# Convolution in eight tiles, a later place for it, and a searched order of all queues, in a hybrid encoder block

## The chip, the cores and the metric

The kernel runs on the 8 cores of one Trainium2 chip. Each core takes one of 8 sequences, and no core talks to another. The time is device microseconds (us) of the slowest core. Some executions fall into a slower state, in which the cores of a die (cores 0 to 3 or 4 to 7) show a lower granted clock. The granted clock is the share of its full clock that TensorE was given. Medians are over all executions.

## The reference, cut to what matters

Per core: 2048 tokens of width 1024. One block does:

```python
x   = layer_norm(x)
u   = x @ W_in            # [q | k | v | conv-GLU halves | gates], 3840 columns
y_a = windowed_gqa(q, k, v) @ W_attn_out     # 8 heads, 128-token blocks, 3 key blocks each
glu = u_a * sigmoid(u_b)                     # 512 channels
dw  = depthwise_conv(glu, width 31) + b      # each channel alone, taps t-15 .. t+15
y_c = silu(layer_norm(dw)) @ W_conv_out
mix = (sigmoid(g_a) * y_a + sigmoid(g_c) * y_c) @ W_out
h   = layer_norm(alpha * x + mix)
out = layer_norm(alpha * h + (silu(h @ W_gate) * (h @ W_up)) @ W_down)   # D_FF = 2816
```

## The kernel before

The kernel is a list of operations. A helper records each with what it reads and writes, an estimated cost and a number called rank. A small list scheduler then simulates the engines: whenever an engine is free, it takes the ready operation of lowest rank. The resulting order of each queue is fixed in the program. Tokens are worked in four chunks of 512.

The convolution runs on TensorE. The GLU output goes to DRAM scratch and comes back as copies shifted by one token each, so that the 128 rows of the array hold 32 channels times 4 shifts, and a matmul of 128 rows by 32 columns applies 4 taps to 32 channels:

```python
def spread(c):                         # four loads of 540 KB for each chunk
    for s in range(4):
        load(shv[32*s:32*s+32, :, :], gs[:, :, c*512+s : c*512+s+GW], ..., rank=0.1*c)

def conv(c):
    for cc in range(4):                # four groups of 128 channels
        b = ring("conv", CONV)         # a fixed few PSUM banks for each purpose
        def f_conv(e, cc=cc, b=b):
            for m in range(8):         # 8 steps of 4 taps
                for q in range(4):     # 4 tiles of 32 columns
                    e.matmul(bank(b)[32*q:32*q+32, :], tapv[:, 4*cc+q, m, :],
                             shv[:, 4*cc+q, 4*m:4*m+512], start=(m == 0), stop=(m == 7))
        ...
for c in range(4):
    rank(100*c - 85); [ln_tile(t) for t in range(4*c, 4*c+4)]
    rank(100*c + 20); glu blocks of chunk c; glu_out(c)
    if c >= 1:
        rank(100*c + 10); spread(c - 1)
        rank(100*c + 35); conv(c - 1)
    rank(100*c + 60); kv(c)
    ...
rank(345); conv(3)
rank(370 + 5*c): q projections;   rank(400 + 20*c), but 330 for chunk 0: attention;   rank(500 + 100*c): gates
```

At the start, the eight weight loads of the GLU wait for x tile 0, and x tile 4 waits for the sixth of them:

```python
wop.append(castload(wA[4 + i], win_d[10 + i], ..., after=[xop[0]]))
xload(t, after=[wop[5]] if t == 4 else [])
```

The softmax here doesn't subtract the row's maximum and nothing guards it: scores larger than these inputs give would overflow.

## Time and profile before

| | before |
|---|---|
| median of 5 executions | 942.27 us (939.13 to 967.92) |
| profiled execution, slowest core (core 5) | 939.7 us; the cores lie between 925.3 and 939.7 |
| TensorE busy, core 5 | 885.1 us, so 54.6 us idle |
| convolution matmuls | 512, busy 34.8 us, with 14.0 us of waits just before them |

TensorE is the bound. The table of windows of core 5 shows where it falls short; its columns are the stretch, its length, then busy us of PE (TensorE), PEld (its weight loads), DVE (VectorE), ACT (ScalarE) and POOL (GpSimd) with their instructions, the granted TensorE clock, the DMA share and GB/s.

```profile
0.00:60.00 60.00, 45.04 (x297) 29.65 (x298) 45.87 (x82) 26.92 (x44) 15.16 (x30) 0.97 0.91 196
60.00:190.00 130.00, 111.84 (x962) 54.38 (x964) 64.33 (x98) 60.85 (x84) 31.06 (x31) 0.93 0.61 118
190.00:345.00 155.00, 147.12 (x1048) 68.94 (x1041) 110.50 (x151) 91.56 (x117) 47.85 (x50) 1.00 0.40 83
345.00:520.00 175.00, 170.81 (x822) 78.67 (x820) 76.20 (x108) 45.10 (x62) 46.63 (x67) 0.98 0.58 100
```

The four stretches leave 15, 18, 8 and 4 us of TensorE idle; from 520 to 900 us it is 1. In the second the clock is down to 0.93, so part of its busy time is slow work as well. That is the stretch of the convolutions.

### The profile page before, as it was taken

How to read it: one execution, taken by the hardware profiler on the slowest of the kernel's cores; microseconds unless marked ns; L12 is line 12 of the kernel's file. 1: busy time of each engine (PE TensorE's matmuls, PEld its weight loads, DVE VectorE, ACT ScalarE, POOL GpSimd, SP SyncE). 2: the span in 40 equal slices, each digit the busy share in tenths (PEclk: the TensorE clock that was granted, in tenths of full speed). 3: DMA queues.
4: the chain of work that ended last, by engine and by line, in shares of the span. 5: the costliest groups of instructions: out<-in, count | busy, mean ns of one | idle time of the engine just before them, and what ended most of it. 6: DMA issues, size and time to landing. Idle time of an engine off the chain costs nothing.

```text
span 939.7 us, 14653 instructions; the slowest of 8 cores (925.3 to 939.7 us)
## 1 busy us (share of the span) xinstructions
PE 885.1 (94%) x5067; PEld 419.2 (45%) x5067; DVE 495.3 (53%) x708; ACT 282.0 (30%) x397; POOL 221.4 (24%) x294
## 2 busy tenths in 40 slices
PE   5897987897999999998999999999999999999996
PEld 2653444443444444443444444444444444444442
DVE  7885324668777574424343386542685443622145
ACT  3562634588565223321222002231003220011100
POOL 3210330551231422334220013320133310233000
PEclk9998998999999999999899999999999999999998
DMA  8965539527034700469982139660258721199201
GB/s 174 213 170 106 116 75 200 98 49 132 1 69 143 148 3 1 90 111 192 171 142 36 35 112 174 107 112 12 91 126 144 126 42 34 46 162 164 44 24 67
DMA packets 46970, 95.43 MB, mean 102 GB/s; under 512 B 5425, under 2 KB 15793, under 8 KB 46641
## 3 DMA queue, kind: packets, MB, share of 16 engines
q0 software_dynamic: 27360, 54.57, 36.3%
q1 hardware_dynamic: 19538, 39.93, 15.9%
q8 instruction: 42, 0.69, 0.3%
q14 instruction: 30, 0.25, 0.1%
HBM read 138.52 MB, written 10.52 MB: 159 GB/s over the span
## 4 chain that ended last, share of the span: by engine, by line
PE 77%; DMA 12%; DVE 4%; issue 3%; SPq 2%; ACT 1%; POOL 0%; DVEq 0%; ACTq 0%; POOLq 0%
PE ps L967 30%; PE ps L985 16%; PE ps L596 13%; PE ps L913 6%; PE ps L862 5%; PE ps L683 3%; DMA sh<-glu_scratch 3%; DMA xE<-x 3%; DMA xt<-x 2%; SPq L479 2%; DMA bias<-biasT 2%; DMA glu_scratch<-glus 2%; DMA wA<-win 1%; PE ps L799 1%; DVE E L471 1%
## 5 line engine op out<-in xcount | busy, mean ns | idle before, releaser
L967 PE MATMUL ps<-mT,wE 128*128 128x512 bf16 x1408 | 310.4, 380 | 0.6 <-DMA wE<-wg 0.6
L967 PEld LDWEIGHTS ps<-mT,wE 128*128 128x128 bf16 x1408 | 137.6, 98 | 165.0 <-issue 2.7
L457 ACT ACTIVATE sgb<-ps 128x512 f32<-128x512 f32 x88 | 52.5, 598 | 384.6 <-PE ps L967 310.0
L985 PE MATMUL ps<-wdn,hid 128*128 128x512 bf16 x704 | 152.6, 379 | 1.0 <-DVE hid L475 1.0
L475 DVE TENSOR_TENSOR hid<-ps,sgb 128x512 bf16<-128x512 f32 x88 | 60.8, 691 | 172.0 <-PE ps L967 153.5
L596 PE MATMUL ps<-x0T,wG 128*128 128x512 bf16 x512 | 118.7, 379 | 0.2 <-ACT gt L457 0.2
L985 PEld LDWEIGHTS ps<-wdn,hid 128*128 128x128 bf16 x704 | 68.8, 98 | 84.3 <-issue 1.5
L471 DVE SCALAR_TENSOR_TENSOR xE<-xE,ps 128x512 f32<-128x512 f32 x64 | 43.9, 686 | 86.1 <-PE ps L985 62.2
L509 POOL TENSOR_TENSOR rs<-mv,neghalf 128x1 f32<-128x1 f32 x28 | 35.1, 1254 | 186.3 <-DVE mv L507 186.3
L596 PEld LDWEIGHTS ps<-x0T,wG 128*128 128x128 bf16 x512 | 48.7, 98 | 60.0 <-issue 4.0
L457 ACT ACTIVATE gt<-ps,hbg 128x512 f32<-128x512 f32 x64 | 43.9, 686 | 87.6 <-PE ps L596 61.0
L471 DVE SCALAR_TENSOR_TENSOR E<-ps,bias 128x1024 f32<-128x1024 f32 x46 | 56.1, 1220 | 20.1 <-PE ps L799 15.6
L471 DVE SCALAR_TENSOR_TENSOR t<-gt,ps 128x512 f32<-128x512 f32 x64 | 43.4, 682 | 43.5 <-ACT gt L457 34.2
L475 POOL TENSOR_TENSOR mT<-t,t 128x512 bf16<-128x512 f32 x32 | 43.4, 1358 | 96.0 <-DVE t L471 76.9
L483 POOL DMA_DIRECT2D wE<-wg x70 | 37.9, 542 | 115.6 <-PE ps L967 103.5
L596 PE MATMUL ps<-x0T,wA 128*128 128x512 bf16 (+1 forms) x320 | 60.1, 346 | 2.6 <-ACT x0T L462 2.5
L913 PE MATMUL ps<-wout,mT 128*128 128x512 bf16 x256 | 58.4, 381 | 0.0
L457 ACT ACTIVATE pT<-E 128x1024 bf16<-128x1024 f32 x46 | 48.3, 1057 | 33.7 <-DVE E L471 33.6
L483 POOL DMA_DIRECT2D wE<-wu x70 | 37.5, 536 | 63.8 <-PE ps L967 55.8
L683 PE MATMUL ps<-sh,tapw 128*32 128x512 bf16 x512 | 34.8, 434 | 14.0 <-DMA sh<-glu_scratch 12.9
L496 DVE BATCH_NORM_STATS2 st<-xE 128x6 f32<-128x512 f32 x64 | 44.4, 694 | 6.1
L596 PEld LDWEIGHTS ps<-x0T,wA 128*128 128x128 bf16 x320 | 31.6, 101 | 27.6 <-issue 4.8
(98 smaller groups left out, 808.7 us busy)
## 6 DMA issues: line engine op xcount, KB each, us to landing
wE<-wg POOLq DMA_DIRECT2D x70, 256.0 KB, 5.6
wE<-wu POOLq DMA_DIRECT2D x70, 256.0 KB, 5.8
sh<-glu_scratch SPq DMA_DIRECT2D x16, 540.0 KB, 10.9
xt<-x SPq DMA_DIRECT2D x16, 512.0 KB, 8.0
xE<-x SPq DMA_DIRECT2D x16, 512.0 KB, 4.5
out<-xE SPq DMA_DIRECT2D x15, 512.0 KB, 2.7
wdn<-wd POOLq DMA_DIRECT2D x11, 512.0 KB, 5.6
wG<-win POOLq DMA_DIRECT2D x16, 256.0 KB, 10.6
```

Source lines behind the costliest of these rows:

```text
L457: sc.add("act", lambda e: e.activation(out, in_, func, **kw), reads=reads, writes=writes, cost=c, table=table, **k)
L471: sc.add("dve", lambda e: e.scalar_tensor_tensor(out, in0, scalar, in1, op0, op1), reads=reads, writes=writes, cost=dcost(n), **k)
L475: sc.add(eng, lambda e: e.tensor_tensor(out, a, b, op), reads=reads, writes=writes, cost=dcost(n) if eng == "dve" else 0.1 + n * 0.0023, **k)
L483: return sc.add("pool", lambda e: e.dma_start(out=dst, in_=src), reads=reads, writes=writes, dma=True, cost=0.6, nbytes=nbytes, **k)
L496: sc.add("dve", lambda e, h=h: e.bn_stats(st[:, 6 * h:6 * h + 6], src[:, 512 * h:512 * h + 512]), reads=[regs[h]], writes=[(sk, h)], cost= ...
L509: sc.add("pool", lambda e: e.tensor_tensor(rs_out, var, neghalf[:, 0:1], ALU.pow), reads=[mreg, "neghalf"], writes=[rreg], cost=0.7)
L596: ins = e.matmul(bank(b)[:, 0:n], w8(w)[:, kc, :], x0v(c)[:, kc, s0:s0 + n], start=(kc == 0), stop=(kc == 7))
L683: ins = e.matmul(bank(b)[32 * q:32 * q + 32, :], tapv[:, 4 * cc + q, m, :], shv[:, 4 * cc + q, 4 * m:4 * m + 512], start=(m == 0), stop=(m ...
L862: ins = e.matmul(bank(b), wv[:, x, f * 128:(f + 1) * 128], src[:, x, :], start=(x == 0), stop=(x == 3))
L913: ins = e.matmul(bank(h), mv[:, kc, tl * 128:(tl + 1) * 128], woutv[:, kc, h * 512:(h + 1) * 512], start=(kc == 0), stop=(kc == 7))
L967: ins = e.matmul(bank(b), w8(wE[i])[:, kc, :], hT[:, kc, :], start=(kc == 0), stop=(kc == 7))
L985: ins = e.matmul(bank(b), hidv[:, k, tl * 128:(tl + 1) * 128], wdnv[k // 2][:, k % 2, h * 512:(h + 1) * 512], start=(k == 0), stop=(k == N ...
```

## The change

The intent is to close the gaps of TensorE in the first 345 us. Five things are done at once.

1. The convolution uses 64 by 32 tiles, eight at a time: two shifts of 32 channels to a half of the rows, sixteen steps. Shifted loads halve to 271 KB. Matmuls come in groups of 32 with two banks.
2. The convolution and the k/v projections (but those of chunk 0) get ranks of 322 to 329, so that the GLU projections go first; the first attention has 330.
3. At the start, weights and x tiles no longer wait for each other, nor the q/k/v weights wQ for those of the GLU; ScalarE takes the statistics of 12 instead of 7 tiles; the GLU of chunks 0 and 1 goes by single tiles of 128 tokens.
4. Banks of PSUM, the memory that the matmuls write to, are picked by the scheduler from all eight, for each tile, instead of from fixed rings; its cost model is finer.
5. A table of 471 numbers, by their look found by a search, replaces or shifts the ranks, and a few loads are moved by hand at the head of the queues.

Smaller parts: the zeros of the padding are set by a memset instead of two strided writes, the convolution's output has a second buffer, and the loads of gate weights wait for the last x tile.

```diff
+RANK = { ("att0", "pe"): 3.31, ("att1", "act"): 1.58, ...      # about 100 lines of searched ranks
+    "conv0": 238.3, "conv1": 315.05, "conv2": 323.77, "conv3": 324.65, ... }
-        op.rank = self.cur if rank is None else rank
+        op.rank = RANK.get(self.group, self.cur) + RANK.get((self.group, eng), 0) if rank is None else rank
@@ start
-        wop.append(castload(wA[4 + i][:, :], win_d[10 + i], ["wA%d" % (4 + i)], after=[xop[0]]))
+        wop.append(castload(wA[4 + i][:, :], win_d[10 + i], ["wA%d" % (4 + i)], wire=1.72))
-            xload(t, after=[wop[5]] if t == 4 else [])
-        if t % 2 and t > 1:
+        if t % 4:
             act_stats(...)
@@ spread: copies for two halves of the rows, two shifts each
+        for h in range(2):
+            for s in range(2):
+                load(shv[64*h+32*s : 64*h+32*s+32, :, lo:hi], gs[:, 8*h:8*h+8, c*512+s+lo : c*512+s+hi], ...)
@@ conv
-            b = ring("conv", CONV)
+        for p in range(2):
+            bs = [T("conv"), T("conv")]
+            for m0 in range(0, 16, 4):
+                def f_conv(e, p=p, bs=bs, m0=m0):
+                    for m in range(m0, m0 + 4):
+                        for q in range(4):
+                            for h in range(2):
+                                e.matmul(pb(bs[h])[32*q:32*q+32, :], tapv[64*h:64*h+64, 4*p+q, m, :],
+                                         shv[64*h:64*h+64, 4*p+q, 2*m:2*m+512], start=(m == 0), stop=(m == 15))
@@ ranks
-            rank(100 * c + 35)
+            stage("conv%d" % (c - 1), 321 + c)
             conv(c - 1)
-        rank(100 * c + 60)
+        stage("kv%d" % c, 326 + c if c else 60)
         kv(c)
-    rank(345)
+    stage("conv3", 325)
     conv(3)
@@ after the scheduler: hand-set heads of queues, and all but 4 of 26 warm-up groups dropped
+    for name, at in {"small": 1, "xt0": 2, "xt1": 3}.items(): move("sp", find("sp", name)[0], at)
+    names = ["wA4", "wA0", ("rsA", 0), "wA5", "wA1", ...]
```

## The prediction

> **What bounds the kernel now.** I read the page first: busy times, then the slices.
>
> ```profile
> PE 885.1 (94%) x5067; PEld 419.2 (45%) x5067; DVE 495.3 (53%) x708; ACT 282.0 (30%) x397; POOL 221.4 (24%) x294
> PE   5897987897999999998999999999999999999996
> DVE  7885324668777574424343386542685443622145
> PEclk9998998999999999999899999999999999999998
> DMA  8965539527034700469982139660258721199201
> ```
>
> TensorE is the bound, but a slice is 23.5 us, and the digits below 9 lie almost all in the first ten slices, that is before about 235 us. Busy time hides pipelining, so I made a second sum from the timeline of TensorE: each group of matmuls at the pace that it keeps where it runs undisturbed (16 matmuls of 512 columns every 3.45 us, so 0.2158 us each; a transpose group of 8 in 0.45; 64 conv matmuls in 3.64; 24 matmuls of attention times V in 0.83; a score pair in 0.32). That sum is about 860 us of needed work without the start-up broadcasts. The span is 939.7, so 79.6 us are idle or slow time. Following start minus accumulated work through the timeline, they lie so: 15.9 before the first transpose; about 9 more by 82 us; 22.6 between 82 and 187 us; about 8 in 187 to 300; about 8 in 300 to 450; under 2 from there to the last matmul; 8.4 after it; the rest is rounding and small gaps. The list of waits of TensorE names the causes:
>
> ```profile
> PE ps L683 <- DMA sh<-glu_scratch: 12.9, 3, 5.2
> PE ps L799 <- DVE E L471: 5.8, 5, 2.4
> PE ps L605 <- DVE mvA L507: 5.7, 1, 5.7
> PE ps L605 <- DVE mvA L519: 4.0, 3, 2.3
> PE ps L605 <- ACT hbb L462: 3.6, 1, 3.6
> ```
>
> Columns are total us, times, longest. The dearest wait is the conv (L683) for its shifted copies. The timeline shows that it costs more than 12.9:
>
> ```profile
> 88.68 9.73 PE L683 MATMUL ps<-sh,tapw 128*32 128x512 bf16 x128 [4.33 <-DMA sh<-glu_scratch]
> ...
> 121.64 8.62 PE L683 MATMUL ps<-sh,tapw 128*32 128x512 bf16 x128 [3.42 <-DMA sh<-glu_scratch]
> ...
> 153.74 3.60 PE L683 MATMUL ps<-sh,tapw 128*32 128x512 bf16 x32 [5.18 <-DMA sh<-glu_scratch]
> ...
> 163.01 3.64 PE L683 MATMUL ps<-sh,tapw 128*32 128x512 bf16 x64
> ```
>
> 64 take 3.64 at full pace, so 128 should take 7.28; after the waits they take 9.73 and 8.62, and 32 take 3.60 where 1.82 would do. The three waits with the slow time after them lose 4.5+2.4, 3.6+1.3 and 5.3+1.7+0.8: 19.6 us.
>
> The start is a chain of issue conditions, as the chain of work that ended last shows: weights wait for the first x tile, and later x tiles for weights.
>
> ```profile
> 1.87 6.97 DMA xt<-x
> 9.39 2.60 POOL wA L483 x5
> 11.99 11.67 DMA wA<-win
> 25.58 11.85 DMA xt<-x
> ```
>
> [...]the granted clock is 0.80 in 90 to 100 us and 0.66 in 150 to 160, after the waits of 4.33 and 5.18 us, and the conv rows above run slow there.[...]no trace yet shows whether eight run together.[...]
>
> **The change part by part.**
> *Conv.* The taps are split two shifts by sixteen steps instead of four by eight, in 64-row by 32-column tiles: 1024 matmuls instead of 512. Now four matmuls share a pass: 3.64/64 = 56.9 ns each, 29.1 us in all. If eight share a pass of 0.2158 us, 1024 need 27.6; at the 34.5 ns of the smallest matmuls now, 35.3. I take +3 us of TensorE time.
> *Spread.* Each of the sixteen shifted loads falls from 32x16x540x2 bytes (the page's 540 KB, 10.9 us to landing) to 32x8x542x2, which is 271 KB. Strided zero writes for the padding (20 us to landing) become a memset. Conv's priority falls behind the next chunk's projections, and its matmuls come in groups of 32 among other work. I let 16 of the 19.6 us go.
> *LayerNorm front.* Weights no longer wait for x tile 0, nor x tile 4 for weights. Statistics of twelve tiles instead of seven go to ScalarE: VectorE loses about 1.6 us (two of 0.68 and 0.2) in five tiles and ScalarE gains 2.5 in each; it was busy about 4 of 10 us there. The GLU of chunks 0 and 1 goes tile by tile, so TensorE can begin with one tile. Against it: 512 matmuls of 128 columns where 192 wider ones stood, at 55.8 ns against 53.9 per 128 columns, so about +1 us; and all eight weights are wanted at once, while the DMA share is already 1.0 in 10 to 20 us. The chain x load 7, statistics, rstd, two passes of 1.28, transpose is untouched: the first transpose stays near 15 us. Of the 9 us lost after that by 82 us I count 4 back.
> *Banks and order.* PSUM banks are picked from all eight by a scheduler instead of a fixed pair for scores; the list of ranks reorders every queue. Score and attention waits, 8 us in 187 to 300: I count 5 back. The 8 us in 300 to 450 wait for x reloads (16.1 us in flight on the chain) behind weight loads; reordering may help, half: 4.
> *Untouched.* Feed-forward matmuls (L967 310.4 and L985 152.6 us busy, almost no idle) and the 8.4 us tail. With 1408+704 of the matmuls at 0.2158, 456 us cannot move.
> *Sum.* 939.7 - 16 - 4 - 5 - 4 + 3 + 1 = 915.7 if each part recovers what I set down. The search behind the ranks should also remove some of the small gaps, and conv waits removed early let the later work close up; the upper end of the recoverable, 19.6+9+8+8 = 44.6 less 4, gives 899. I set the span at 905, between them and nearer the lower, since the ranks look like a search over just these waits. The measured time is 942.27 where this span is 939.7; adding 2 gives **907 us**, 3.7% less.
>
> **The rivals.**
> A: *The wait moves.* [...]a fixed order fitted to one timing can stall elsewhere[...]: spans now run from 925.3 to 939.7 us with the same program. Also VectorE is 0.85 to 1.0 busy in 30 to 80 us, so faster loads may only expose LayerNorm. For: those busy shares. Against: five tiles' statistics leave it. Half the gain would be kept: 922 to 928.
> B: *The conv does not pack.* If eight tiles do not run together, 1024 matmuls at 56.9 ns are 58.3 us, +29: 930 to 940. For: the score pairs, two 64-row matmuls, take 0.32 us rather than 0.216, so packing of rows has an overhead here. Against: 0.32 is below twice 0.216, so they do overlap. If a row switch costs that 0.1 us only once per group of 32, the 32 groups add 3 us.
> C: *Nothing is left idle.* The packed order leaves only the 15 us start and the 8.4 us tail: 860 + 4 + 24 plus 5[...], 893 + 2 = 895.
> D: *Denser work lowers the clock.* Against: granted clock is 1.00 through the dense 460 to 900 us. I give it little.
>
> **Range and chances.** C sets the lower side and A the upper: 891 to 925. The 2% line lies at 923.4. A at its worst, or B, crosses it; a slower kernel needs B with new waits. Faster 0.83, same 0.14, slower 0.03.
>
> **What would show it.** Right: no wait of conv for its shifted copies above 2 us in total; their loads 271 KB and landing in about 6 us; conv busy about 30 us; the granted clock 1.0 from 60 us on; TensorE idle about 25 us instead of 54.6; the feed-forward groups unchanged within 1%. Wrong steps: first transpose later than 17 us (weights in front of x); conv pace above 40 ns (packing); a wait of transposes for LayerNorm, or of attention for VectorE, above 10 us (rival A); idle in 300 to 450 still 5 us (x reloads untouched). If TensorE idle falls as said but the time does not, the pace of the dense part changed, and the reasoning on the clock is what failed.

## The result, and the profile after

| | before | after |
|---|---|---|
| median | 943.92 us, 17 executions (939.13 to 1077.02) | 919.98 us, 9 executions (918.02 to 981.88) |
| ratio of fast runs | | 0.975, 95% interval 0.9727 to 0.9773 |
| profiled execution, slowest core | 939.7 us | 916.6 us (core 0) |

Of the 9 executions after, one was slow (981.88). A ratio is the mean time of one kernel's fast runs over that of the other's fast runs of the same rounds, so it is not quite the ratio of the medians that are quoted. The kernel is 2.5% faster. The prediction said 3.7%, with a range that holds the result.

Core 0's records lack 89 matmuls, so the lines below are of core 7, which has all 5904 and ended at 916.0 us. First its page: busy time, then the slices.

```profile
PE 878.7 (96%) x5904; PEld 424.7 (46%) x5904; DVE 493.8 (54%) x701; ACT 291.4 (32%) x414; POOL 204.5 (22%) x287
PE   6899999999999999998999999999999999999996
PEclk9999999999999999999999999999999999999999
DMA  8939282380212470489993146931367642199201
```

TensorE's row is 9 from the third slice to the last but one, except for one 8, and no slice has a clock below 9. Idle time is 916.0 - 878.7 = 37.3 us instead of 54.6. The table of windows of core 7, cut as before:

```profile
0.00:60.00 60.00, 47.56 (x571) 39.81 (x572) 46.27 (x77) 34.67 (x58) 16.07 (x32) 0.97 0.84 197
60.00:190.00 130.00, 125.23 (x1697) 60.83 (x1695) 82.20 (x115) 85.28 (x117) 29.55 (x34) 1.00 0.54 100
190.00:345.00 155.00, 151.40 (x986) 70.61 (x985) 100.29 (x135) 73.34 (x97) 41.74 (x42) 1.00 0.35 72
345.00:520.00 175.00, 170.81 (x838) 78.95 (x837) 78.52 (x119) 40.29 (x54) 43.44 (x69) 1.00 0.65 109
```

The second stretch gains 13.4 us of busy time, at a clock of 1.00 instead of 0.93; the third gains 4.3, the first 2.5, the fourth nothing. The waits of TensorE (us in total, times, longest):

```profile
PE ps L1286 <- DMA wE<-wg: 4.3, 4, 2.8
PE ps L944 <- DMA wA<-win: 3.8, 2, 2.1
PE ps L1012 <- DVE dsum L750: 3.4, 4, 1.2
```

The convolution is line 989 now and not among them. Its group, by form, and its matmuls in the timeline:

```profile
L989 PE MATMUL ps<-sh,tapw 64*32 64x512 bf16 x1024 | 31.3, 377 | 0.6 <-DMA sh<-glu_scratch 0.5
```

```profile
92.44 1.06 PE L989 MATMUL ps<-sh,tapw 64*32 64x512 bf16 x32
...
119.21 3.65 PE L989 MATMUL ps<-sh,tapw 64*32 64x512 bf16 x128
```

Eight tiles do run together. In the run at 119.21 us the trace has eight starts within 23 ns, 3 ns apart, and the next eight 216 ns later, which is the pace of one matmul of 512 columns on the whole array. So 1024 matmuls need 27.6 us where they run on. They take more because each visit to the convolution costs about 0.2 us: the first start comes 0.09 us late, and the next other matmul 0.11 us late. There are 19 visits on this core.

To compare whole runs I took a second sum from the trace's matmul starts as in the prediction: the distance from each start to the next, less the undisturbed pace of that form (a start every 216 ns for 512 columns, while a record of such a matmul is 379 ns long). I call the rest *lost*; it holds idle and slow time alike. The table gives means over the six cores of each profile whose records are complete. Each row adds up to the mean span of those cores, with 1.5 us before the first matmul.

| mean us | needed work | lost to 60 us | 60 to 190 | 190 to 345 | 345 to 520 | 520 to last start | end | span |
|---|---|---|---|---|---|---|---|---|
| before | 864.8 | 19.2 | 22.5 | 10.3 | 3.8 | 1.2 | 8.6 | 931.9 |
| after | 866.4 | 17.4 | 7.8 | 3.1 | 4.6 | 2.5 | 8.7 | 912.0 |
| difference | +1.6 | -1.8 | -14.7 | -7.2 | +0.8 | +1.3 | +0.1 | -19.9 |

The slowest core gained 23.1 us, from 939.7 to 916.6, more than the mean, since the cores now lie within 8.9 us of each other (907.7 to 916.6) instead of 14.4.

### The profile page after: what moved, and what is told of

Same layout as the page of the kernel before. It is cut to its first block, busy times and chain, and to the rows that moved or that the text cites. A ratio compares the mean times of both kernels' runs of the same rounds, so it can differ in the third digit from the quotient of the medians.

```text
span 916.6 us, 16074 instructions; the slowest of 8 cores (907.7 to 916.6 us)
## 1 busy us (share of the span) xinstructions
PE 873.8 (95%) x5815; PEld 425.4 (46%) x5904; DVE 493.9 (54%) x701; ACT 291.2 (32%) x414; POOL 204.5 (22%) x287
## 3 DMA queue, kind: packets, MB, share of 16 engines
q1 hardware_dynamic: 14530, 35.49, 13.7%
## 4 chain that ended last, share of the span: by engine, by line
PE 73%; DMA 12%; DVE 6%; issue 4%; ACT 3%; POOL 0%; SPq 0%; DVEq 0%; ACTq 0%; POOLq 0%
PE ps L1286 27%; PE ps L1304 17%; PE ps L878 12%; PE ps L1180 4%; PE ps L1234 4%; DMA xE<-x 3%; DMA wE<-wg 3%; PE ps L944 3%; DVE xE L746 2%; DMA sh<-glu_scratch 2%; PE ps L989 2%; DMA wout<-wout 2%; DMA glu_scratch<-glus 2%; PE ps L888 1%; PE ps L1111 1%
## 5 line engine op out<-in xcount | busy, mean ns | idle before, releaser
L1286 PE MATMUL ps<-mT,wE 128*128 128x512 bf16 x1377 | 306.7, 379 | 6.3 <-DMA wE<-wg 3.7
L784 POOL TENSOR_TENSOR rs<-mv,neghalf 128x1 f32<-128x1 f32 x28 | 31.1, 1110 | 179.0 <-DVE mv L782 179.0
L746 DVE SCALAR_TENSOR_TENSOR xE<-xE,mv,lnB 128x1024 f32<-128x1024 f32 (+1 forms) x33 | 42.2, 1282 | 2.7 <-DVE mv L782 0.2
L746 DVE SCALAR_TENSOR_TENSOR xE<-xE,rs,lnB 128x1024 f32<-128x1024 f32 x31 | 39.6, 1278 | 6.4 <-POOL rs L784 4.2
L944 PE MATMUL ps<-x0T,wA 128*128 128x128 bf16 x512 | 34.7, 233 | 6.7 <-ACT x0T L737 3.3
```

Of the source, the lines that this page charges most:

```text
L746: sc.add("dve", lambda e: e.scalar_tensor_tensor(res(out), res(in0), scalar, res(in1), op0, op1), reads=reads, writes=writes, cost=dcost(n ...
L784: sc.add("pool", lambda e: e.tensor_tensor(rs_out, var, neghalf[:, 0:1], ALU.pow), reads=[mreg, "neghalf"], writes=[rreg], cost=0.7)
L944: ins = e.matmul(pb(b)[:, cc * 128:(cc + 1) * 128], w8(wA[w])[:, kc, :], x0v(c)[:, kc, tl * 128:(tl + 1) * 128], start=(kc == 0), stop=(kc ...
L1286: ins = e.matmul(pb(b), w8(wE[i])[:, kc, :], hT[:, kc, :], start=(kc == 0), stop=(kc == 7))
```

## The experiments

My theory after the result: the gain is the convolution's waits with the slow clock after them, removed by its new place in the order, and the waits of attention and gates in 190 to 345 us, removed by banks and searched ranks. Rivals: the halved loads or the eight tiles remove the convolution's waits; the freed start is what helps; the search does nothing that the hand-written ranks don't. Each run stands beside runs of the kernel before on the same chip. That kernel's median varies by chip between 942.88 and 946.09 us in these runs, so times are compared by ratio. The table collects the losses worked out as above; differences under about 4 us in it show nothing by themselves.

| run | ratio to before, interval | lost to 60 | 60 to 190 | 190 to 345 | 345 to 520 |
|---|---|---|---|---|---|
| conv_only | 1.0066, 1.0022 to 1.0111 | 29.5 | 15.8 | 15.1 | 5.1 |
| conv_late | 0.9814, 0.9782 to 0.9845 | 19.8 | 5.9 | 12.0 | 4.8 |
| front_only | 1.0156, 1.0116 to 1.0196 | 26.8 | 32.4 | 12.8 | 4.7 |
| no_ranks | 0.9938, 0.9894 to 0.9982 | 17.7 | 9.8 | 18.1 | 5.4 |
| conv_small | 0.9935, 0.9907 to 0.9962 | 19.5 | 13.4 | 18.6 | 5.2 |
| conv_small_late | 0.9821, 0.9793 to 0.9849 | 20.6 | 7.0 | 11.7 | 4.4 |
| keep_warm | 1.0012, 0.9991 to 1.0033 | 20.3 | 14.6 | 10.7 | 3.9 |
| after_again | 0.9751, 0.9725 to 0.9778 | 17.6 | 8.2 | 3.9 | 4.7 |
| ffn_loads | 0.9754, 0.9735 to 0.9773 | 17.5 | 8.3 | 3.2 | 6.2 |
| all_warm | 0.9764, 0.9744 to 0.9784 | 10.8 | 7.3 | 2.8 | 3.9 |
| x_later | 0.9835, 0.9813 to 0.9857 | 25.5 | 8.1 | 3.0 | 4.8 |
| weights_wait | 0.9761, 0.9739 to 0.9783 | 17.8 | 10.0 | 3.2 | 5.7 |

**conv_late**: the kernel before, with part 2 of the change alone.

```diff
-            rank(100 * c + 35)
+            rank(321 + c)
             conv(c - 1)
-        rank(100 * c + 60)
+        rank(326 + c if c else 60)
         kv(c)
-    rank(345)
+    rank(325)
     conv(3)
```

> The kernel before with only the priority of the conv and of the key and value projections lowered, to the base values of the change; loads stay at 540 KB. If the order is what removes the waits: conv waits under 3 us, granted clock 1.0 from 90 to 190 us, time 925 to 932. If the loads' size is: the waits stay or move to attention (which needs the same projections), and the time is within 5 us of before.

Measured: median 926.36 us, ratio 0.9814. These three lines bring 1.9% of the 2.5%. The timeline of TensorE, to be read against the rows of line 683 in the prediction:

```profile
102.82 7.09 PE L683 MATMUL ps<-sh,tapw 128*32 128x512 bf16 x128
113.46 1.91 PE L683 MATMUL ps<-sh,tapw 128*32 128x512 bf16 x32
```

On none of the eight cores does a convolution wait for its copies (12.9 us on core 5 before), 128 matmuls take 7.09 us instead of 9.73, and the loads are still of 540 KB. The first convolution merely starts at 102.82 instead of 88.68, behind 80 GLU matmuls that were ready. Lost time in 60 to 190 us falls from 22.5 to 5.9. The run moves the convolution and the k/v projections together; which of the two counts was not separated. All the rest of the change, its search included, adds the 0.6% that are left.

**conv_only**: part 1 alone, each chunk's convolution in two groups of 128 matmuls, a group into two banks.

```diff
-            for m in range(8):
-                for q in range(4):
-                    ins = e.matmul(bank(b)[32*q:32*q+32, :], tapv[:, 4*cc+q, m, :], ...)
+            for m in range(16):
+                for q in range(4):
+                    for h in range(2):
+                        ins = e.matmul(bank(bs[h])[32*q:32*q+32, :], tapv[64*h:64*h+64, 4*p+q, m, :], ...)
-    sh, _ = sbn(RG, 2, [128, 16 * GW], BF16, "sh")
+    sh, _ = sbn(RG, 2, [128, 8 * GW], BF16, "sh")
```

> The kernel before with the conv re-tiled alone (64x32 tiles, halved shifted loads, pads by memset), its own order and priorities kept. If the loads' size made the conv wait: landing of the shifted loads falls from 10.9 to about 6.5 us, the conv's three waits (12.9 us and the slow clock after them, 19.6 in all) fall to under 6, and the time is 928 to 934. If the place in the order made it wait (conv first in the queue, whatever the size), the waits stay above 8 us and the time is within 5 us of before. If eight tiles do not pack, the conv's busy time is over 45 us and the time rises.

Measured: 950.18 us, ratio 1.0066: 0.7% slower, with the interval above 1. The cause is a side effect. The smaller buffers left memory free, so seven loads of gate weights lost the dependency that had held them back, and the old scheduler put them first. The timeline of GpSimd, which issues them:

```profile
2.25 3.71 POOL L483 DMA_DIRECT2D wG<-win  x7
8.25 2.65 POOL L483 DMA_DIRECT2D wA<-win  x5 [2.29 <-DMA xt<-x]
```

The GLU weights wA, wanted first, then took 19.6 us in the median from issue to landing instead of 10.0. So the run can't tell what tiles and loads are worth. The changed kernel does not have this fault: there these loads wait for the last x tile.

**conv_small**: the same with the old size of the buffers kept, so that the order of loads stays.

```diff
-    sh, _ = sbn(RG, 2, [128, 8 * GW], BF16, "sh")          # of conv_only
+    sh, _ = sbn(RG, 2, [128, 16 * GW], BF16, "sh")
+    shv = sh[c % 2][:, 0:8 * GW].rearrange("p (r t) -> p r t", r=8)
```

> The re-tiled conv with halved loads again on the kernel before, this time with the old size of the buffers kept, because in the run conv_only the freed memory let gate weights be loaded at 2 us, ahead of everything. If smaller loads help by themselves: start as before (lost 13 to 14 us between 16 and 60 us), the conv's waits fall from 12.9 to under 8 us and the time by 5 to 10 us, to 933 to 938. If the place in the order is all: within 5 us of before (943).

Measured: 938.98 us, ratio 0.9935. The wait of the convolution stays, at 7.4 us instead of 12.9:

```profile
PE ps L808 <- DVE E L471: 7.8, 4, 3.2
PE ps L688 <- DMA sh<-glu_scratch: 7.4, 3, 2.6
```

The eight tiles with their halved loads and the memset together help by 0.65% on the slowest core. In the profiled execution nearly all that the mean core gains in 60 to 190 us (22.5 to 13.4) is lost again in 190 to 345 (10.3 to 18.6), where attention now waits longer for VectorE (the first line).

**conv_small_late**: conv_small and conv_late together (both diffs above).

> The same with the lowered priority of the run conv_late added. If the order alone removes the waits, the halved loads add nothing to conv_late (926 us, ratio 0.981): 923 to 929. If the load's size is worth something of its own, 915 to 920.

Measured: 928.49 us, ratio 0.9821. By form, the convolution's group:

```profile
L688 PE MATMUL ps<-sh,tapw 64*32 64x512 bf16 x1024 | 29.2, 375 | 0.2 <-DVE den L475 0.2
```

The interval overlaps that of conv_late. With the convolution late, halved loads and eight tiles add nothing that can be seen. Busy time of 29.2 us, against 31.3 in the changed kernel, shows the price of that kernel's shorter groups: 8 visits instead of 19, by starts in the trace of one core each.

**keep_warm**: the kernel before, with 28 small matmuls on constants ahead of the first convolution group of each chunk. It was meant to take away the slow clock and leave the wait for the data.

```diff
+    for o in [o for o in sc.ops["pe"] if getattr(o.fn, "__name__", "") == "f_conv0"]:
+        ... p = _Op("pe", f_dummy, False)      # 28 matmuls 128x256, into the bank of the group
+        p.deps = {d: True for d in o.deps if not d.dma}
+        sc.ops["pe"].insert(sc.ops["pe"].index(o), p)
```

> The kernel before with 28 idle matmuls (128x256, results overwritten) put right ahead of each chunk's first conv, so that TensorE stays active through its waits for the shifted copies; nothing else moves. If the half clock after the waits is a loss of its own, as I read the trace (2.4, 1.3 and 2.5 us), the granted clock is near 1.0 from 90 to 160 us, 128 conv matmuls take about 7.3 us, and the time falls by 3 to 6 us. If it is not, the time is unchanged or up by the 3 us each that the idle matmuls take where no wait is.

Measured: 946.95 us, ratio 1.0012: no gain. The timeline:

```profile
89.61 7.09 PE L684 MATMUL ps<-sh,tapw 128*32 128x512 bf16 x128 [0.85 <-DMA sh<-glu_scratch]
121.98 8.78 PE L684 MATMUL ps<-sh,tapw 128*32 128x512 bf16 x128 [2.40 <-DMA sh<-glu_scratch]
154.79 3.60 PE L684 MATMUL ps<-sh,tapw 128*32 128x512 bf16 x32 [5.74 <-DMA sh<-glu_scratch]
```

The first convolution, with 0.85 us of idle time left, takes 7.09 us at a granted clock of 1.00 (88 to 100 us), so its 9.73 us before was slow work after the wait, at a clock of 0.50 in 88 to 93 us. The two others kept waits of 2.40 and 5.74 us after the 28 matmuls, and stay slow, with the granted clock at 0.83 in 120 to 130 us and 0.69 in 150 to 160. That slow work goes when the wait goes is shown at one place; what the clock costs in all is not measured, because the added matmuls need about 4 x 28 x 0.108 = 12.1 us themselves, an estimate from half the pace of 512 columns (0.2158 us); a record of the 28 is 3.22 us long in the timeline.

**front_only**: part 3 without the GLU by tiles, on the kernel before.

```diff
-        wop.append(castload(wA[i][:, :], win_d[6 + i], ["wA%d" % i], after=[xop[0]]))
+        wop.append(castload(wA[i][:, :], win_d[6 + i], ["wA%d" % i]))
-        castload(wQ[i][:, :], win_d[ch], ["wQ%d" % i], rank=50 if i < 2 else 60, after=[wop[7]])
+        castload(wQ[i][:, :], win_d[ch], ["wQ%d" % i], rank=50 if i < 2 else 60)
-            xload(t, after=[wop[5]] if t == 4 else [])
-        if t % 2 and t > 1:
+            xload(t)
+        if t % 4:
```

> The kernel before with only the front changed: weights no longer wait for x tile 0, x tile 4 no longer for weights, statistics of 12 tiles instead of 7 on ScalarE. My account from the two traces gives the whole front 1 to 3 us (lost time to 60 us 20.6 before, 18.2 after): time 938 to 943. The rival, that the chain x tile, weights, x tile of the chain of waits was worth its length, gives 930 to 935.

Measured: 958.56 us, ratio 1.0156, 1.6% slower, which neither of my expectations had. The eight wA are issued from 2.2 us on, four of the six wQ right behind them at 6.37, and all share the transfer with the x tiles (DMA share 0.86 in the first 16 us): wA then lands 17.2 us after issue in the median, instead of 10.0. The waits of TensorE tell the rest:

```profile
PE ps L683 <- DMA sh<-glu_scratch: 17.9, 3, 6.6
PE ps L799 <- DVE E L471: 10.2, 6, 4.5
PE ps L605 <- DVE mvA L519: 8.2, 2, 6.9
PE ps L605 <- DVE mvA L498: 6.7, 1, 6.7
```

Transposes (line 605) wait for statistics of x tiles that come late, 6.9 and 6.7 us, and the order fitted to other times then makes the convolution wait 17.9 us. Freed waits at the start are no gain by themselves: under this order the conditions that I read as needless in the chain acted as a throttle. Whether wA or wQ held the x tiles up was not separated; in the changed kernel the wQ stand behind LayerNorm work in the queue of GpSimd.

**weights_wait**: the changed kernel with that condition put back for the eight weights.

```diff
+    for n in ["wA%d" % i for i in range(8)]:
+        find("pool", n)[0].deps[xop[0]] = True
```

> The changed kernel with one thing undone: the eight GLU weights wait for the first x tile again, as in the kernel before; order, banks and all else stay. In the changed kernel the first transpose comes at 13.65 us and the last GLU weight lands at 35.1 us; 17 to 18 us of TensorE time are lost up to 60 us. Theory (the front edit is worth little by itself, because x tiles and weights share one saturated wire): the first transpose comes no later than 13.7 us or a little earlier, all weights shift by the 3 to 4 us that x tile 0 needs, the loss up to 60 us changes by no more than 3 us, the time stays within 0.4 per cent of the changed kernel: 916 to 922, ratio to the kernel before 0.973 to 0.978. Rival (the free start of the weights carries the front gain of about 4 us that the prediction booked): the loss up to 60 us grows by 4 us or more and the time is 922 to 926, ratio 0.979 to 0.983. The conv waits should stay under 2 us under both, because the searched order holds the conv back.

Measured: 922.31 us, ratio 0.9761, where the changed kernel had 0.975. From the timeline of GpSimd and the waits of TensorE, both of the slowest core:

```profile
7.28 1.20 POOL L758 DMA_DIRECT2D wA<-win  x2 [6.58 <-DMA xt<-x]
PE ps L989 <- DMA sh<-glu_scratch: 4.8, 2, 3.8
```

The first weight is issued at 7.28 us instead of 4.81, and the first transpose comes at 13.64 us, as without the condition (13.68). Lost time to 60 us is 17.8 against 17.4. So the free start of the weights is worth nothing that can be seen here; x tile 4 stayed free. The median is 0.3 us over the upper limit that I gave for the first theory; the ratio is inside it. One sign failed: the convolution waits 4.8 us on this core, where I had said under 2 (1.2 on core 5). Why the first transpose moved from 15.91 to 13.68 us is then left to the order of the first loads and of VectorE's first operations, which was not undone singly.

**x_later**: the changed kernel with x tiles 3 and 4 held until weights wA1 and wA2 have landed, the opposite trade.

```diff
+    xop[3].deps[find("pool", "wA1")[0]] = True
+    xop[4].deps[find("pool", "wA2")[0]] = True
```

> The changed kernel with x tile 3 held until the fourth gated-linear weight has landed and x tile 4 until the sixth; nothing else moves. The last of these eight weights lands at 35 us in the changed kernel, 26 us before, since weights and x tiles share the wire. If the front is bound by that sharing: the last weight lands before 31 us and the loss between 16 and 60 us falls from 12 to 8 or 10. If LayerNorm's own pace bounds it: the later tiles make TensorE wait for them instead, and the time is the same or up to 3 us longer.

Measured: 927.75 us (one of five executions was slow), ratio 0.9835, so by the ratio 8 us are lost again, more than either expectation had. By core, the last weight lands at 25 to 29 us instead of 32 to 35, but the third transpose moves from about 25 us to 30 and later (33.56 on the slowest core). The timeline of TensorE on that core:

```profile
21.11 1.01 PE L888 MATMUL ps<-ident,x0b 128*128 128x128 bf16 x8 [0.57 <-DVE mvA L794]
32.75 1.01 PE L944 MATMUL ps<-x0T,wA 128*128 128x128 bf16 x8 [10.63 <-ACT x0T L737]
```

One wait of 10.63 us takes the place of several of 2: the copy of the second tile, transposed by 22 us, stands behind the statistics of the held x tile 3 in ScalarE's queue, and ScalarE waits 9.36 us for that tile. Weights and x tiles share one busy transfer (DMA share 1.03 in 8 to 28 us on core 7 of the changed kernel): what one got early in these two runs, the other got late. The split in the changed kernel is the better of the two.

**all_warm**: the changed kernel without the dropping of warm-up groups (26 groups instead of 4).

```diff
-    for o in [o for o in Q["pe"] if o.vts and o.vts[0].kind == "warm"][4:]:
-        drop(o)
```

> The changed kernel with all 26 groups of warm-up matmuls kept, where it drops all but 4: 66 more small matmuls before 30 us. If the slow clock in the first 16 us of useful work is what the front still loses, the granted clock there rises and the time falls by 1 to 3 us. If the warm-ups stand in the way of the first transpose (13.7 us), it starts 1 to 4 us later and the time rises by as much.

Measured: 919.58 us, ratio 0.9764, the same. Lost time to 60 us falls from 17.4 to 10.8, but that is the added matmuls filling idle time: needed work grows by 7.1 us. On five of the eight cores the first transpose comes at 16.8 to 17.5 us instead of 13.3 to 13.7, and the time is still the same. Nor does the clock at the start decide which core is late: in the changed kernel it is 0.50 in 8 to 28 us on cores 3, 4 and 6 and 1.00 on the others, and cores 4 and 6 are among the early ones (909.2 and 908.9 us), core 3 is not (914.8).

**no_ranks**: the changed kernel with an empty table of ranks, so hand-written ranks under the new scheduler.

```diff
-RANK = { ("att0", "pe"): 3.31, ... }
+RANK = {}
```

> The kernel after with the table of searched ranks emptied, so the scheduler orders by the stages' base ranks. If the parts (smaller loads, free banks, finer conv groups) carry the gain: 920 to 928. If the search carries it: 935 or more, with waits of TensorE back above 30 us.

Measured: 937.84 us, ratio 0.9938. The loss lies in one stretch: 190 to 345 us, 18.1 us instead of 3.1. That stretch in the table of windows of core 7:

```profile
190.00:345.00 155.00, 140.69 (x975) 67.01 (x974) 115.49 (x160) 82.38 (x103) 37.37 (x40) 0.94 0.35 69
```

TensorE is idle for 14.3 us of it, and its clock falls to 0.94. The timeline there has many waits of 0.2 to 2.9 us on VectorE's and ScalarE's attention work. The table of ranks removes them. So the gain of 60 to 190 us needs no table, and the rest of the change under hand-written ranks is worse in attention than the kernel before (18.1 against 10.3 us). Which part does that is not shown: banks, scheduler, shorter convolution groups and start all differ, and conv_small_late, with fixed banks, has 11.7. Nor can I split the 7.2 us that remain: the ranks go with those banks.

**after_again**: the changed kernel once more, on the chip of the three runs next named. No edit.

> The changed kernel itself, unaltered, as the yardstick for the three variants of it on the same chip: ratio 0.973 to 0.977 of before.

Measured: 918.18 us, ratio 0.9751. It is the yardstick for ffn_loads, all_warm and x_later.

**ffn_loads**: the changed kernel with the last three loads of down-projection weights and one of LayerNorm constants moved behind the gate and up weights.

```diff
+    late = [o for o in Q["pool"] if o.dma and str(o.w[0]).startswith("wdn")][-3:]
+    ...
+    Q["pool"][at - 2:at - 2] = late
+    o.deps[find("dve", ("hid", 12))[0]] = True            # o: the load of lnB2
```

> The changed kernel with three loads of down-projection weights and the load of the second norm's parameters moved behind the gate and up weights around 408 to 450 us; nothing else moves. In the changed kernel those four (some 4 MB) share the wire with the weights that TensorE then waits for (3 to 4 us lost between 411 and 450 us on most cores). If that order is the new wait: the loss there falls under 1.5 us and the time by 2 to 4 us against the changed kernel. If the wire is simply full for the whole stretch: the waits move a few us later and the time is within 1 us.

Measured: 918.8 us, ratio 0.9754, the same. In the changed kernel the feed-forward part starts with a wait at 424.92 us; here waits come some 40 us later. First the timeline of the changed kernel (core 7), then of ffn_loads (core 3):

```profile
424.92 3.61 PE L1286 MATMUL ps<-mT,wE 128*128 128x512 bf16 x16 [2.82 <-DMA wE<-wg]
429.63 5.34 PE L1286 MATMUL ps<-mT,wE 128*128 128x512 bf16 x24 [1.09 <-DVE xE L746]
```

```profile
461.75 5.34 PE L1286 MATMUL ps<-mT,wE 128*128 128x512 bf16 x24 [2.45 <-DMA wE<-wg]
470.96 20.53 PE L1286 MATMUL ps<-mT,wE 128*128 128x512 bf16 x88 [3.88 <-DMA wE<-wg]
```

The DMA share of the changed kernel is 1.05 in 411 to 440 us and 1.08 in 440 to 470. The transfer itself is full there, and this reordering moved the wait and did not remove it.

No version beat the changed kernel.

## Why the prediction was right or wrong

**Bound and place of the gain: right.** TensorE was the bound, and all the loss that went, 23.7 us on the mean core, lay before 345 us. The feed-forward matmuls stayed as they were: the mean record is 380 and 379 ns long before, 379 and 379 after.

**Convolution, -16: size right, cause misread.** Lost time in 60 to 190 us fell by 14.7. I gave the gain to halved loads and the later place together. Conv_late shows that the later place alone does it (22.5 to 5.9), with loads of 540 KB, and conv_small_late that halved loads add nothing to that. What I wrote of the slow work after a wait held: keep_warm shows it at the first convolution, and conv_late has 7.09 us for what took 9.73. The signs that I had named came: a wait for copies of 0.6 us, loads of 271 KB that land in 7.3 (core 7), a clock of 1.00.

**Eight tiles, +3: right in effect.** They run together, (3.65 - 1.06) / 96 = 27.0 ns each in a long run, so rival B failed. My remark there, that a switch might cost 0.1 us for each group, was the right kind of cost: 0.2 us for each of 19 visits. It is the same whether a visit holds 32 matmuls or 128, and a visit to the 128 by 32 tiles costs as much in the kernel before, where no wait stands ahead of it (at 197.58 us: the first start 0.09 us late, the next other matmul 0.1). The four tiles of a pass start 3 to 4 ns apart there, and in conv_late they give (7.09 - 1.91) / 96 = 54.0 ns a matmul, twice the 27.0.

**Front, -4: size wrong, reason wrong.** It is -1.8 in the table, too little to be sure of. Removing the condition on the weights does nothing in the changed kernel (weights_wait), and removing all of them costs 1.6% on the old order (front_only). I had named the full transfer (DMA share 1.04 in 10 to 20 us, core 5 before) as the argument against it and counted 4 us all the same. The first transpose, which I left near 15 us, came at 13.68.

**Banks and order, -5: right, a little small.** It is -7.2 in 190 to 345 us. I had not seen that the other parts need the table of ranks there: without it the loss is 18.1.

**x reloads, -4: wrong.** The loss in 345 to 520 us is 3.8 before and 4.6 after. On core 5 before, TensorE waited 3.62 us at 447 us behind a reload that was 16.09 us in flight. After, core 7 waits 2.82 us for gate weights where the feed-forward part starts, and the chain that ended last on core 0 still holds a reload of 14.90 us. This is rival A, the moved wait, in a small way; ffn_loads moved it once more and gained nothing.

**The step that failed is the last one of the sum.** The terms add up to -25, so to a span of 914.7; I wrote 915.7, a slip of 1. The mean core gained 19.9 us (reloads and front too hopeful by 7, convolution by 1, the stretch after 520 us not counted, 1; ranks too shy by 2, work set 2 too high), the slowest 23.1, to 916.6. The sum with its 2 us for the metric was 917, and 919.98 was measured; that it comes so close is partly luck, since errors of 9 us one way and 5 us the other partly cancel. But then I set the span at 905, "since the ranks look like a search over just these waits". Those 10 us had to come out of the 15.6 that the terms had left in the 44.6 of losses, and no term said which. The runs show in its place that the ranks gain in one stretch, 15 us, and that about half of this undoes what the rest of the change loses there under hand-written ranks. What stays idle, 37.3 us on core 7 and not 25, is mostly the start (some 17 us lost), the end (8.7) and waits where the transfer is full (DMA share 1.05 in 411 to 440 us, 1.08 in 440 to 470). None of the orders that I tried made these smaller.

**Chances.** Denser work did not lower the clock (rival D): from 60 us to the last matmuls it is 1.00 on core 7, and 0.83 only for 10 us near 425 on cores 5 and 6, around a wait. Rival C left 29 us lost, where the table has 44: 17.4 at the start, 18.0 from 60 us to the last start, 8.7 at the end.

**Open.** How the 7.2 us divide between banks and ranks; which of the first loads moved the first transpose; why cores differ by 9 us with one program (in both profiles one core of each pair 0 and 1, 2 and 3, 4 and 5, 6 and 7 ends 3 to 13 us after the other); and about 3 us by which the mean core gained less than the slowest, which may be chance of one execution.

## What to carry to other kernels

When a queue's order is fixed and its head waits for data, look first for ready work that could stand ahead of the waiting group; here three changed ranks gave 1.9%, and halving the transfer gave nothing on top. A condition that delays a load may be what keeps a full transfer in a useful order (without such conditions front_only was 1.6% slower, with the GLU weights 17.2 us in flight instead of 10.0), so test its removal alone before counting it as gain. Keep a forecast to its terms: what no row of the profile carries should not be added at the end.
